# Fourteen pairs instead of thirteen in the down projection of a hybrid decoder layer

## The chip, the cores and the metric

The kernel runs on one core of one Trainium2 chip. The core has five engines with a queue of instructions each: TensorE (PE, matrix products; PEld is its loading of the stationary operand), VectorE (DVE), ScalarE (ACT), GpSimd (POOL) and SyncE (SP), which here issues nearly all DMA transfers. The metric is the device time of one execution in microseconds (us), and the median over several executions is what counts. Matrix products are summed in eight PSUM banks; everything else lies in SBUF, 128 partitions wide.

## The reference

One decoder layer in fp32 over 256 positions of width 2048:

```python
h    = rmsnorm(x, pre_mix_gain)
proj = h @ w_in                                   # 2048 x 6144
o_sb = head_rmsnorm(stick_breaking_attention(q_sb, k_sb, v_sb))        # 8 heads
o_dl = head_rmsnorm(dilated_attention(rope(q_dl), rope(k_dl), v_dl))   # 8 heads
x    = x + rmsnorm(concat(o_sb, o_dl) @ w_out, post_mix_gain)
h    = rmsnorm(x, pre_ffn_gain)
u    = causal_conv3(h @ w_up) + conv_b            # 2048 x 11008
y    = gelu(u[:, :5504]) * u[:, 5504:]
x    = x + rmsnorm(y @ w_down, post_ffn_gain)     # 5504 x 2048
```

What concerns the change is the last product, `y @ w_down`: 43 blocks of 128 along the 5504 rows, each against 2048 columns, for two blocks of 128 positions.

## The kernel before, in words

**Products in parts.** A weight arrives in fp32 (`raw`, a ring of five buffers of 128 × 1024), ACT rounds it to its high part `wh` (L88), and DVE subtracts that to get the low part `wl` (L93); both have rings of four. The activations are split in the same way. Each product is then three matmuls into one bank: high by high, low by high, high by low (in down L621, L622, L623).

**Stages.** v and qk with the attention of the heads between them, out, up, down, in this order on PE. In each of the first 55 steps behind the seventh, `presum` is called once (L895).

**Down.** The output has two column halves (`cp` 0 and 1) of 1024 columns. A half takes the 43 blocks of rows in two ways. A *single* (`ONE`) is one block: four products, 12 matmuls, one raw tile of 1024 columns. A *pair* (`PAIR`) is two blocks by a scheme of the Strassen kind: seven products instead of eight, 21 matmuls. It has four units: Rb (two products), Ra (one, 512 wide), T13 and T24 (two each). T13 is a sum of weights that `presum` has formed during attention: it loads two pieces of `w_dn` (b12 and t13), adds them on DVE (L575) and writes the result to DRAM (`t13_kept`), from where down reads it as any weight. T24 is formed in down by two additions of 512 columns on DVE (L604, L606). The activations of a pair (`yp`, seven matrices) are formed in up, those of a single (`yt`) as well. `prepare` runs three units ahead of `multiply`.

The order comes from `_down_plan`: with 13 pairs there are 17 singles. Half 0 opens with two singles, then pairs with singles spread between them (rounded down), and both halves end with four singles (`HELD`). In half 0 pairs 0 and 1, and 6 and 7, stand side by side; in half 1 a single follows each pair. Where the order isn't written out, the framework places each instruction on its engine; `pin` and `keep_in_program_order` fix it.

**Between and behind the halves.** `combine` (L630 to L634) adds the pairs' products of banks 1, 5, 6 and 7; `close` (L641) adds a bank of singles to that, ACT squares the sum for the last norm (L436), and the result is scaled by the gain `gbc` (L643). In half 1 the four held singles run bank by bank (2, 3, 4, and 8 in two pieces), so that each bank is closed while PE works on the next; L680 (`put`) applies the norm and adds x1, and SP writes the output. `x1p` is a piece of x1 that ACT copies to PSUM (L693) for it.

**Small things.** `along_rows` (L311) turns a column of factors into rows by a product with a matrix of ones; it is used in the first norm and, behind the first pieces of up, in the second (`r2ps`). Up's `convolved` computes a gate and a value in the tiles `cv0` and `cv1`; a pair's sums lie in the tile `pair`.

Of the kernel before, what the change touches and what calls it, by code (L numbers as in the profile page):

```python
# [16 lines left out]
P = 128  # L17
D = 2048
S = 256
# [14 lines left out]
NPAIR = 13  # L34
# [17 lines left out]
def layer_kernel(ctx: ExitStack, tc: tile.TileContext, a, out: bass.AP):  # L52
# [12 lines left out]
    def pin(ins):  # L65

        if pinned[0]:
            tc.keep_in_program_order(ins)
        return ins
# [81 lines left out]
    def rstd_of(v, n):  # L151

        l = small.tile([P, n], F32, tag=f"rl{n}", name="rl")
        A.activation(l, v, AF.Ln)
        r0 = small.tile([P, n], F32, tag=f"r0{n}", name="r0")
        A.activation(r0, l, AF.Exp, scale=-0.5)
        q = small.tile([P, n], F32, tag=f"rq{n}", name="rq")
# [3 lines left out]
        r = small.tile([P, n], F32, tag=f"rr{n}", name="rr")  # L161
        V.tensor_tensor(r, r0, q, op=ALU.mult)
        return r
# [131 lines left out]
    ones = cpool.tile([P, P], F32, name="ones")  # L295
    G.memset(ones, 1.0)
# [8 lines left out]
    def along_rows(r, name):  # L305

        ps = ps_at.tile([P, S], F32, tag="at", name=name)
        for t in range(2):
            dg = small.tile([P, P], F32, tag="diag", name="diag", bufs=1)
            V.tensor_scalar(dg, ident, r[t], None, op0=ALU.mult)  # L310
            T.matmul(ps[:, t * P:(t + 1) * P], ones, dg, start=True, stop=True)  # L311
        return ps

    def first_norm():

        V.tensor_copy(tri, cst[:, C_TRI:C_TRI + P])
        G.tensor_copy(idb, ident)
        G.tensor_copy(mskb, cst[:, C_MSK:C_MSK + P])
        ss = small.tile([P, 2], F32, tag="ssx", name="ssx", bufs=1)
        for t in range(2):  # L320
            A.activation(gbc, x1[:, t, :], AF.Square, accum_out=ss[:, t:t + 1])
        v0 = small.tile([P, 2], F32, tag="vx", name="vx", bufs=1)
        V.tensor_scalar(v0, ss, 1.0 / D, EPS, op0=ALU.mult, op1=ALU.add)
        V.tensor_copy(rstd1, rstd_of(v0, 2))
        rps = along_rows((rstd1[:, 0:1], rstd1[:, 1:2]), "rps")
# [9 lines left out]
    def finish_head(h, at, den):  # L335
# [7 lines left out]
        hs = small.tile([P, 2], F32, tag="hs", name="hs")  # L343
# [3 lines left out]
        v = small.tile([P, 2], F32, tag="hv", name="hv")  # L347
        if den is None:
            V.tensor_scalar(v, hs, 1.0 / P, EPS, op0=ALU.mult, op1=ALU.add)
        else:  # L350

            e2 = small.tile([P, 2], F32, tag="e2", name="e2")
# [42 lines left out]
    def dilated_head(h, qk):  # L395
# [12 lines left out]
        m = small.tile([P, 2], F32, tag="m", name="m")  # L408
        den = small.tile([P, 2], F32, tag="den", name="den")
# [77 lines left out]
    def convolved(ps, p, s):  # L487
# [5 lines left out]
        cv = phB.tile([P, S], F32, tag=f"cv{s}", name="cv", bufs=1)  # L493
# [6 lines left out]
        else:  # L500
            m, odd = p // (FT // NPAIR), p % (FT // NPAIR)
            if p in SINGLES:
                n = SINGLES.index(p)
                V.tensor_tensor(cv, gate[0], cv, op=ALU.mult)
# [3 lines left out]
            if odd == 0:  # L508
                pair[0] = phB.tile([P, 7, P], F32, tag="pair", name="pair", bufs=1)
            y = pair[0]  # L510
            V.tensor_tensor(y[:, 2 * odd:2 * odd + 2, :], gate[0], cv, op=ALU.mult)
# [9 lines left out]
    class Down:  # L521
# [42 lines left out]
        def presum(self, tick):  # L564


            pair, odd = divmod(tick, 2)
            if not odd and 0 <= pair - 2 < len(self.presums):
                t13, _, kept = self.summed[pair - 2]
                tc.keep_in_program_order(nc.sync.dma_start(kept, t13))  # L570
            if odd and 0 <= pair - 1 < len(self.presums):
                t13, one, _ = self.summed[pair - 1]
# [3 lines left out]
            if not odd and pair < len(self.presums):  # L576
# [68 lines left out]
        def run(self):  # L645
# [254 lines left out]
    V.tensor_scalar(gbc, gbc, -0.5, None, op0=ALU.mult)  # L900
# [75 lines left out]
```

## Time and profile before

| | |
|---|---|
| median of three runs | 1117.7 us (1117.26 to 1117.78) |
| profiled execution: its own time | 1117.35 us |
| its span | 1115.6 us |
| granted clock | 0.998 |
| PE busy | 1103.6 us, 5855 matmuls |
| DVE, ACT busy | 880.6 us, 659.1 us |

By the trace, attention runs to about 312 us, the output projection to 397, up from 414 to 887.9, half 0 of down to 997.35, half 1 to the last matmul at 1106.8, and the last output leaves by 1115.6.

The rows in the prediction are of these kinds. A timeline row has the start, the duration, engine, line, operation, output <- inputs, shapes and how many equal ones it stands for; brackets name the idle time ahead of it and what ended it. A group row has a shape, its count, busy time and mean nanoseconds of one, then the engine's idle time ahead of such instructions and its releasers. A row of waits has the total, the number and the longest. A row of windows has, behind the stretch and its length, each engine's busy time with its instructions, then PE's clock, the share of DMA and GB/s.

### The profile page before, as it was taken

The numbers are of one execution on the slowest core, as the hardware profiler recorded it, in microseconds if no ns is written. First come the engines' busy times: TensorE is split into PE (matmuls) and PEld (weight loads), VectorE is DVE, ScalarE is ACT, GpSimd is POOL, SyncE is SP. The second block draws the span as 40 slices with busy tenths as digits, with TensorE's granted clock in tenths as the row PEclk, the third lists the DMA queues.
The fourth block names the chain that finished last, engine by engine and source line by source line (L and its number), as shares of the span: only waits on it lengthen the run. The fifth ranks groups of instructions, "written<-read, shape, count | busy, mean of one in ns | idle before, by whom it ended". The sixth has DMA issues, their size and how long they took to land.

```text
span 1115.6 us, 16305 instructions
## 1 busy us (share of the span) xinstructions
PE 1103.6 (99%) x5855; PEld 941.3 (84%) x5855; DVE 880.6 (79%) x1373; ACT 659.1 (59%) x1041; POOL 3.3 (0%) x10
## 2 busy tenths in 40 slices
PE   9999999999999999999999999999999999999996
PEld 6888888888888888888888888888888888888885
DVE  6577776777776589878888878888878898889887
ACT  6656665655654376655555555555555566666664
POOL 0000000000000000000000000000000000000000
PEclk9999999999999999999999999999999999999999
DMA  9977778878879756555555555555555577777775
GB/s 319 369 254 272 256 250 269 300 251 277 274 259 320 274 199 211 189 189 189 189 189 185 188 184 187 185 188 187 188 189 189 173 252 244 249 223 246 245 238 206
DMA packets 75393, 257.79 MB, mean 231 GB/s; under 512 B 8496, under 2 KB 9648, under 8 KB 74544
## 3 DMA queue, kind: packets, MB, share of 16 engines
q1 hardware_dynamic: 75168, 256.74, 68.9%
q8 instruction: 46, 0.75, 0.3%
q14 instruction: 35, 0.29, 0.1%
q10 hardware_dynamic: 144, 0.01, 0.0%
HBM read 238.89 MB, written 17.83 MB: 230 GB/s over the span
## 4 chain that ended last, share of the span: by engine, by line
PE 98%; DVE 0%; DMA 0%; ACT 0%; issue 0%; DVEq 0%; SPq 0%; ACTq 0%
PE mmu L101 28%; PE mmu L104 14%; PE mmqk L101 11%; PE p L622 7%; PE p L621 7%; PE p L623 6%; PE mmqk L104 5%; PE mmv L144 3%; PE mmv L147 3%; PE mmo L143 3%; PE mmv L143 3%; PE mmo L144 3%; PE mmo L147 3%; PE mmu L110 1%; DMA raw<-in_w_v 0%; PE po L341 0%
## 5 line engine op out<-in xcount | busy, mean ns | idle before, releaser
L88 ACT CAST wh<-raw 128x1024 fp32r<-128x1024 f32 (+1 forms) x408 | 415.1, 1024 | 356.4 <-PE mmu L101 190.1
L93 DVE TENSOR_TENSOR wl<-raw,wh 128x1024 fp32r<-128x1024 f32 (+1 forms) x408 | 482.5, 1189 | 165.2 <-ACT wh L88 160.6
L101 PE MATMUL mmu<-hT,wh 128*128 128x512 f32 x1344 | 340.9, 396 | 0.0
L101 PEld LDWEIGHTS mmu<-hT,wh 128*128 128x128 f32 x1344 | 240.2, 188 | 45.6
L104 PEld LDWEIGHTS mmu<-hT,wl 128*128 128x128 f32 x1344 | 182.8, 189 | 15.2
L104 PE MATMUL mmu<-hT,wl 128*128 128x256 f32 x1344 | 186.4, 281 | 0.0
L101 PE MATMUL mmqk<-hT,wh 128*128 128x512 f32 x512 | 133.0, 401 | 0.0
L101 PEld LDWEIGHTS mmqk<-hT,wh 128*128 128x128 f32 x512 | 92.0, 188 | 17.2
L104 PEld LDWEIGHTS mmqk<-hT,wl 128*128 128x128 f32 x512 | 69.9, 188 | 5.8
L622 PE MATMUL p<-wh,yp 128*128 128x512 f32 x182 | 71.7, 394 | 0.0
L621 PE MATMUL p<-wh,yp 128*128 128x512 f32 x182 | 71.3, 392 | 0.0
L104 PE MATMUL mmqk<-hT,wl 128*128 128x256 f32 x512 | 71.1, 281 | 0.0
L623 PE MATMUL p<-wl,yp 128*128 128x512 f32 x182 | 70.8, 389 | 0.0
L622 PE MATMUL p<-wh,yt 128*128 128x512 f32 (+1 forms) x140 | 54.2, 387 | 0.0
L621 PE MATMUL p<-wh,yt 128*128 128x512 f32 (+1 forms) x140 | 54.0, 385 | 0.0
L623 PE MATMUL p<-wl,yt 128*128 128x512 f32 (+1 forms) x140 | 53.3, 382 | 0.0
L494 ACT ACTIVATE cv<-u,par 128x256 f32<-128x256 f32 x86 | 51.5, 598 | 2.4 <-DVE u L492 2.3
L143 PE MATMUL mmv<-wh,hT 128*128 128x512 f32 x128 | 51.6, 405 | 0.4 <-ACT hT L225 0.4
L144 PE MATMUL mmv<-wh,hT 128*128 128x512 f32 x128 | 50.8, 397 | 0.2 <-DVE hT L226 0.2
L143 PE MATMUL mmo<-wh,mix 128*128 128x512 f32 x128 | 50.4, 394 | 0.0
L88 ACT CAST wh<-room 128x1024 fp32r<-128x1024 f32 x26 | 27.3, 1050 | 38.6 <-PE p L622 36.4
L144 PE MATMUL mmo<-wh,mix 128*128 128x512 f32 x128 | 49.9, 390 | 0.0
(175 smaller groups left out, 1218.6 us busy)
## 6 DMA issues: line engine op xcount, KB each, us to landing
raw<-in_w_up SPq DMA_DIRECT2D x172, 512.0 KB, 4.4
raw<-in_w_qk SPq DMA_DIRECT2D x64, 512.0 KB, 4.9
raw<-in_w_dn SPq DMA_DIRECT2D x60, 512.0 KB, 4.6
raw<-in_w_o SPq DMA_DIRECT2D x32, 512.0 KB, 5.0
raw<-in_w_v SPq DMA_DIRECT2D x28, 512.0 KB, 5.6
t<-in_w_dn SPq DMA_DIRECT2D x26, 512.0 KB, 5.7
t_kept<-t SPq DMA_DIRECT2D x26, 512.0 KB, 3.9
raw<-t_kept SPq DMA_DIRECT2D x26, 512.0 KB, 4.4
```

Of the source, the lines that this page charges most:

```text
L88: pin(A.copy(wh, raw))
L93: pin(V.tensor_tensor(wl, raw, wh.bitcast(F32), op=ALU.subtract))
L101: T.matmul(ps, wh[:, j * P:(j + 1) * P], h[:, k, :, :], start=(k == 0), stop=False, skip_group_check=True)
L104: T.matmul(ps[:, 0, :], wl[:, j * P:(j + 1) * P], h[:, k, 0, :], start=False, stop=(k == KT - 1), skip_group_check=True)
L110: T.matmul(ps[:, part, :], parts[k // 8][low][:, k % 8 * P:(k % 8 + 1) * P], h[:, k, part, :], skip_group_check=True, **kw)
L143: T.matmul(ps[t], hi[:, k, tc_], ws, start=(first and i == 0 and j == 0), stop=False)
L144: T.matmul(ps[t], lo[:, k, tc_], ws, start=False, stop=False)
L147: T.matmul(ps[t], hi[:, k, tc_], wl[:, j * 512:(j + 1) * 512], start=False, stop=(last and i == len(parts) - 1 and j == n - 1))
L494: A.activation(cv, u, AF.Identity, scale=cw(2), bias=par[:, P_CB + f:P_CB + f + 1])
L621: T.matmul(ps, yh, wh[:, cs], start=key not in self.begun, stop=False)
L622: T.matmul(ps, yl, wh[:, cs], start=False, stop=False)
L623: T.matmul(ps, yh, wl[:, cs], start=False, stop=self.left[key] == 0)
```

## The change

- NPAIR goes from 13 to 14, so 15 singles are left in each half. Half 0 opens with three singles, and the others are spread by rounding up: side by side stand now pairs 2 and 3, 4 and 5, 6 and 7, 9 and 10, 11 and 12 in half 0, 4 and 5 and 9 and 10 in half 1, and in both halves the last pair stands directly ahead of the four held singles.
- `presum` spreads 28 sums over 52 steps with its own lags, instead of one per two steps.
- The attention's small tiles (`rl`, `r0`, `rq`, `rr`, `hs`, `hv`, `e2`, `m`, `den`) move from the pool `small`, which lives to the end, to `apool`, which ends ahead of up. Both have four buffers for them.
- `ones` and the diagonal share one tile of the early pool, and for the second norm a new tile is taken in the buffer `pair`, and POOL fills it again.
- Up's value half lies inside the tile `pair`, and its gate in a tile of its own.
- The gain's scaling by −0.5 moves from ahead of down to the middle of half 0.
- The copies `x1p` move ahead of the products of bank 3.

```diff
-NPAIR = 13
+NPAIR = 14
+SUM_STEPS = 52
...
-    plan = [("one", left.pop(0)) for _ in range(0 if cp else 2)]
+    plan = [("one", left.pop(0)) for _ in range(0 if cp else 3)]
     spread = len(left) - HELD
     for m in range(NPAIR):
         plan.append(("pair", m))
-        plan += [("one", left.pop(0)) for _ in range((m + 1) * spread // NPAIR - m * spread // NPAIR)]
+        plan += [("one", left.pop(0)) for _ in range(-(-(m + 1) * spread // NPAIR) + (-m * spread // NPAIR))]
...
-        l = small.tile([P, n], F32, tag=f"rl{n}", name="rl")
+        l = apool.tile([P, n], F32, tag=f"rl{n}", name="rl", bufs=4)
...
-    ones = cpool.tile([P, P], F32, name="ones")
-    G.memset(ones, 1.0)
+    ones = apool.tile([P, 2 * P], F32, name="ones", bufs=1)
+    G.memset(ones[:, 0:P], 1.0)
...
-            dg = small.tile([P, P], F32, tag="diag", name="diag", bufs=1)
+            dg = ones[:, P:2 * P]
             V.tensor_scalar(dg, ident, r[t], None, op0=ALU.mult)
-            T.matmul(ps[:, t * P:(t + 1) * P], ones, dg, start=True, stop=True)
+            T.matmul(ps[:, t * P:(t + 1) * P], ones[:, 0:P], dg, start=True, stop=True)
...
         rs = [sq.newton(*sq.mean(t)) for t in range(2)]
+        ones = phB.tile([P, 2 * P], F32, tag="pair", name="ones", bufs=1, padded_shape=[P, 7 * P])
+        G.memset(ones[:, 0:P], 1.0)
         r2B = cpool.tile([P, S], F32, name="r2B")
-        V.tensor_scalar(r2B, along_rows(rs, "r2ps"), -0.5, None, op0=ALU.mult)
+        V.tensor_scalar(r2B, along_rows(rs, "r2ps", ones), -0.5, None, op0=ALU.mult)
...
-        cv = phB.tile([P, S], F32, tag=f"cv{s}", name="cv", bufs=1)
+        m, odd = p // (FT // NPAIR), p % (FT // NPAIR)
+        if s == 0:
+            cv = phB.tile([P, S], F32, tag="gate", name="gate", bufs=1)
+        else:
+            if p in SINGLES or odd == 0:
+                pair[0] = phB.tile([P, 7, P], F32, tag="pair", name="pair", bufs=1)
+            at = 0 if p in SINGLES else 2 * odd
+            cv = pair[0][:, at:at + 2, :].rearrange("p a b -> p (a b)")
...
-            pair, odd = divmod(tick, 2)
-            if not odd and 0 <= pair - 2 < len(self.presums):
-                t13, _, kept = self.summed[pair - 2]
+            def due(lag):
+                n, k = len(self.presums), tick - lag
+                return next((p for p in range(n) if SUM_STEPS * p // n == k), None)
+
+            pair = due(3)
+            if pair is not None:
+                t13, _, kept = self.summed[pair]
                 tc.keep_in_program_order(nc.sync.dma_start(kept, t13))
...
                     self.prepare(u + 1 + self.AHEAD)
+                    if cp == 0 and u == n // 2:
+                        tc.keep_in_program_order(V.tensor_scalar(gbc, gbc, -0.5, None, op0=ALU.mult))
                     self.multiply(u)
...
             take2(V)
+            pinned[0] = True
+            for i in range(2):
+                pin(A.copy(x1p[i], x1s[1][:, i * 512:(i + 1) * 512]))
             products(3)
             take3 = self.close(1, 3)
-            for i in range(2):
-                A.copy(x1p[i], x1s[1][:, i * 512:(i + 1) * 512])
-            pinned[0] = True
...
-    V.tensor_scalar(gbc, gbc, -0.5, None, op0=ALU.mult)
```

In the changed kernel the lines of down stand further on: L94 is the subtraction L93 of before, L616 and L618 are L604 and L606, L633 to L635 are the matmuls L621 to L623, L643 to L646 the combining additions, L653 `close`, L655 the scaling by the gain, L667 the scaling of `gbc`, L680 the subtraction of bank 8, L694 `put`.

The first place is DVE in the middle of half 0, where pairs 6 and 7 stand side by side in both kernels. Before (`wl<-room` is the low part of T24, `wl<-raw` of 512 columns that of Ra):

```order
L93 TENSOR_TENSOR wl<-raw,wh 128x1024
L93 TENSOR_TENSOR wl<-room,wh 128x1024
L604 TENSOR_TENSOR room<-raw 128x512
L93 TENSOR_TENSOR wl<-raw,wh 128x1024
L93 TENSOR_TENSOR wl<-raw,wh 128x512
L606 TENSOR_TENSOR room<-room,raw 128x512
L93 TENSOR_TENSOR wl<-raw,wh 128x1024
L93 TENSOR_TENSOR wl<-room,wh 128x1024
L93 TENSOR_TENSOR wl<-raw,wh 128x1024 x2
L604 TENSOR_TENSOR room<-raw 128x512
```

and in the changed kernel, from the last unit of pair 7 on:

```order
L94 TENSOR_TENSOR wl<-raw,wh 128x1024
L94 TENSOR_TENSOR wl<-room,wh 128x1024
L667 TENSOR_SCALAR room<-room 128x2048
L94 TENSOR_TENSOR wl<-raw,wh 128x1024 x2
L616 TENSOR_TENSOR room<-raw 128x512
L94 TENSOR_TENSOR wl<-raw,wh 128x512
```

Between T24 of pair 7 and the single behind it the scaling of the gain now stands.

The second place is DVE at the end of half 1, from the first low part behind T24 of the last pair (`room` is the result, `p6`, `p5`, `p7`, `p2`, `p8`, `p3` are banks). Before:

```order
L93 TENSOR_TENSOR wl_10716<-raw_10649,wh_10714 128x1024
L93 TENSOR_TENSOR wl_10723<-raw_10658,wh_10721 128x1024
L93 TENSOR_TENSOR wl_10733<-raw_10708,wh_10731 128x1024
L631 TENSOR_TENSOR room_9005<-p6_9932,room_9005 128x512
L93 TENSOR_TENSOR wl_10748<-raw_10710,wh_10746 128x1024
L632 TENSOR_TENSOR room_9005<-p5_9930,room_9005 128x512
L633 TENSOR_TENSOR room_9005<-p7_9931,room_9005 128x512
L93 TENSOR_TENSOR wl_10764<-raw_10712,wh_10762 128x1024
L634 TENSOR_TENSOR room_9005<-p5_9930,room_9005 128x512
L641 TENSOR_TENSOR room_9005<-p2_9936,room_9005 128x512
L666 TENSOR_TENSOR room_9005<-room_9005,p8_9937 128x512
L643 TENSOR_TENSOR room_9005<-room_9005 128x512
```

and now:

```order
L94 TENSOR_TENSOR wl_10735<-raw_10670,wh_10733 128x1024
L94 TENSOR_TENSOR wl_10742<-raw_10679,wh_10740 128x1024
L94 TENSOR_TENSOR wl_10752<-raw_10729,wh_10750 128x1024
L643 TENSOR_TENSOR room_8990<-p6_9926,room_8990 128x512
L94 TENSOR_TENSOR wl_10767<-raw_10731,wh_10765 128x1024
L644 TENSOR_TENSOR room_8990<-p5_9924,room_8990 128x512
L653 TENSOR_TENSOR room_8990<-p2_9930,room_8990 128x512
L645 TENSOR_TENSOR room_8990<-p7_9925,room_8990 128x512
L646 TENSOR_TENSOR room_8990<-p5_9924,room_8990 128x512
L655 TENSOR_TENSOR room_8990<-room_8990 128x512
L680 TENSOR_TENSOR room_8990<-room_8990,p8_9931 128x512
L653 TENSOR_TENSOR room_8990<-p3_9929,room_8990 128x512
```

Five low parts stood here, the first that of a single; now there are the four of the held units. Two of the combining additions stand behind the closing of bank 2, and the scaling ahead of the subtraction of bank 8.

More of the change, by code (lines that the diff above doesn't have):

```diff
@@ L160, in rstd_of @@
         V.tensor_scalar(q, q, -0.5, 1.5, op0=ALU.mult, op1=ALU.add)
-        r = small.tile([P, n], F32, tag=f"rr{n}", name="rr")
+        r = apool.tile([P, n], F32, tag=f"rr{n}", name="rr", bufs=4)
         V.tensor_tensor(r, r0, q, op=ALU.mult)
@@ L324, in first_norm @@
         V.tensor_copy(rstd1, rstd_of(v0, 2))
[L325 removed]
+        rps = along_rows((rstd1[:, 0:1], rstd1[:, 1:2]), "rps", ones)
         V.tensor_scalar(rB[:, 0, :], rps, SCALE, None, op0=ALU.mult)
@@ L342, in finish_head @@
         T.matmul(po[:, 1, :], at[:, 2 * P:3 * P], vt[:, 1, hc], start=False, stop=True)
-        hs = small.tile([P, 2], F32, tag="hs", name="hs")
+        hs = apool.tile([P, 2], F32, tag="hs", name="hs", bufs=4)
         for t in range(2):
@@ L346, in finish_head @@
             A.activation(jk, po[:, t, :], AF.Square, accum_out=hs[:, t:t + 1])
-        v = small.tile([P, 2], F32, tag="hv", name="hv")
+        v = apool.tile([P, 2], F32, tag="hv", name="hv", bufs=4)
         if den is None:
@@ L350, in finish_head @@
         else:
-            e2 = small.tile([P, 2], F32, tag="e2", name="e2")
+            e2 = apool.tile([P, 2], F32, tag="e2", name="e2", bufs=4)
             V.scalar_tensor_tensor(e2, den, EPS, den, op0=ALU.mult, op1=ALU.mult)
@@ L564, in presum @@
         def presum(self, tick):
-            pair, odd = divmod(tick, 2)
-            if not odd and 0 <= pair - 2 < len(self.presums):
-                t13, _, kept = self.summed[pair - 2]
+            def due(lag):
[4 more added lines that the diff above has]
+                t13, _, kept = self.summed[pair]
                 tc.keep_in_program_order(nc.sync.dma_start(kept, t13))
-            if odd and 0 <= pair - 1 < len(self.presums):
-                t13, one, _ = self.summed[pair - 1]
+            pair = due(2)
+            if pair is not None:
+                t13, one, _ = self.summed[pair]
                 b12 = one.rearrange("p (o c) -> p o c", o=1).broadcast_to([P, 2, 512])
@@ L575, in presum @@
                 tc.keep_in_program_order(V.tensor_tensor(two, b12, two, op=ALU.add))
-            if not odd and pair < len(self.presums):
+            pair = due(0)
+            if pair is not None:
                 one, two, kept = self.presums[pair]
```

16 lines of the change are left out of this document (6 added, 10 removed).

## The prediction

> **What bounds the kernel now.** First the page: busy time, granted clock by slice, and the chain that ended last.
>
> ```profile
> span 1115.6 us, 16305 instructions
> PE 1103.6 (99%) x5855; PEld 941.3 (84%) x5855; DVE 880.6 (79%) x1373; ACT 659.1 (59%) x1041; POOL 3.3 (0%) x10
> ...
> PEclk9999999999999999999999999999999999999999
> ...
> PE 98%; DVE 0%; DMA 0%; ACT 0%; issue 0%; DVEq 0%; SPq 0%; ACTq 0%
> ```
>
> TensorE is busy or being fed nearly all the time, its clock is full, and the chain is PE for 98%. A busy share of 99% can hide short stalls, so I read next what PE waited for:
>
> ```profile
> PE idle L234 <- DVE warm L231: 1.2, 1, 1.2
> PE pth L803 <- DVE x L795: 1.2, 1, 1.2
> ```
>
> The one wait above 1 us behind the start is at the step from the output projection to up. In down there is none of that size. So the time is the number of matmuls times their pitch, plus what DVE does alone at the end. The pitch is not the mean duration. In the PE timeline a single (12 matmuls) and a pair (21) lie between these starts:
>
> ```profile
> 918.38 0.39 PE L621 MATMUL p<-wh,yt 128*128 128x512 f32 x1
> ...
> 921.13 0.39 PE L621 MATMUL p<-wh,yp 128*128 128x512 f32 x1
> ...
> 925.94 0.39 PE L621 MATMUL p<-wh,yt 128*128 128x512 f32 x1
> ```
>
> A single takes 2.75 us and a pair 4.81 us: 0.229 us a matmul, though each row says 0.39, because neighbours overlap.
>
> **Matmuls removed: −1.37 us.** The groups by line and shape:
>
> ```profile
> L621 PE MATMUL p<-wh,yp 128*128 128x512 f32 x182 | 71.3, 392 | 0.0
> ...
> L621 PE MATMUL p<-wh,yt 128*128 128x512 f32 x132 | 51.7, 392 | 0.0
> ```
>
> One pair more in each column half makes the pair products 196 (28 × 7); two singles fewer in each make the single ones 132 − 16 = 116. Per line that is 2 fewer, on three lines 6, and 6 × 0.229 = 1.37 us. With 0.39 one would write 2.3 us, which the pitch forbids.
>
> **The opening of down: −0.24 us.** DVE (L900, L93), ACT (table load) and PE there:
>
> ```profile
> 887.93 0.40 PE L621 MATMUL p<-wh,yt 128*128 128x512 f32 x1
> ...
> 897.10 0.40 PE L622 MATMUL p<-wh,yp 128*128 128x512 f32 x1
> 897.42 0.51 PE L623 MATMUL p<-wl,yp 128*128 128x512 f32 x1
> 897.77 0.40 PE L621 MATMUL p<-wh,yp 128*128 128x512 f32 x1
> ...
> 898.47 0.39 PE L621 MATMUL p<-wh,yp 128*128 128x512 f32 x1
> ```
> ```profile
> 893.23 1.22 DVE L900 TENSOR_SCALAR room<-room 128x2048 f32<-128x2048 f32 x1
> ...
> 896.15 1.23 DVE L93 TENSOR_TENSOR wl<-room,wh 128x1024 fp32r<-128x1024 f32 x1
> ```
> ```profile
> 893.77 1.28 ACT L902 ACT_TABLE_LOAD   x1
> ```
>
> From 887.93 to 898.47 lie two singles and a pair: 45 × 0.229 = 10.30 us, but it takes 10.54. The lost 0.24 is the low part of pair 0's last unit, ready at 896.15 + 1.23 = 897.38, just as PE asks for it. A third single puts 2.75 us of PE work ahead of that unit against 1.14 us of DVE work (cadence below), and the 1.22 us gain scaling L900 is gone from there. I take the whole 0.24; bounds 0 and 0.24.
>
> **The new memset and the diagonal: +0.15 us.** POOL now fills `ones` again in the second norm.
>
> ```profile
> 420.93 0.42 PE L311 MATMUL r2ps<-diag,ones 128*128 128x128 f32 x2
> ```
> ```profile
> 416.38 0.19 ACT L436 ACTIVATION_READ_ACCUMULATOR jks<-x 128x1 f32 x1
> ```
> ```profile
> L296 POOL MEMSET ones<- x1: 206/206/206, 0.9 to 0.9; 128x128 f32 x1
> ```
>
> The tile takes the buffer of the squares' scratch, so the memset waits for the last square, 416.57, and takes 0.2 us as at the start. PE reads it at 420.93: 4.2 us of cover, and POOL has nothing else queued there. If the cover were gone, PE would stand for the lateness. But the matmul now waits on more semaphores, the last being the diagonal's own, and the PE queue behind it is the up stage. No row prices that; bounds 0 and 0.3, I take the middle.
>
> **Attention and up: 0.** Two more presums are two more of these additions, and 2.6 MB more traffic (768 KB in and 512 KB out, twice):
>
> ```profile
> L575 DVE TENSOR_TENSOR t<-b,t 128x1024 f32<-128x1024 f32 x26 | 31.7, 1220 | 0.0
> ```
> ```profile
> 0.00:312.00 312.00, 310.24 (x1683) 263.75 (x1684) 219.03 (x390) 187.57 (x356) 1.14 (x8) 1.00 0.81 282
> 414.00:887.90 473.90, 473.90 (x2699) 412.70 (x2698) 392.73 (x644) 279.65 (x422) 0.00 (x0) 1.00 0.58 189
> ```
>
> In the attention stage DVE is busy 219 of 312 us and DMA 81%, so 2.4 us and 1% more bytes find room; DVE is the cover, and without it PE would lose the 2.4 us. The small tiles keep four buffers. In up, DVE's 393 of 474 us covers the extra pair's sums, and the half and the sum now live in the buffer that the sum alone had, behind readers that have long ended.
>
> **Down's steady state: +0.05 us.** The place with two pairs side by side and no single between them exists once in the middle of before:
>
> ```profile
> 937.34 1.23 DVE L93 TENSOR_TENSOR wl<-room,wh 128x1024 fp32r<-128x1024 f32 x1 [0.87 <-ACT wh L88]
> ...
> 942.70 1.23 DVE L93 TENSOR_TENSOR wl<-room,wh 128x1024 fp32r<-128x1024 f32 x1
> ...
> 997.23 1.88 DVE L641 TENSOR_TENSOR room<-p,room 128x512 f32<-128x512 f32 x3
> ...
> 1090.53 3.50 DVE L93 TENSOR_TENSOR wl<-raw,wh 128x1024 fp32r<-128x1024 f32 x3 [0.22 <-ACT wh L88]
> ```
> ```profile
> 940.13 0.39 PE L623 MATMUL p<-wl,yp 128*128 128x512 f32 x1
> ...
> 944.94 0.39 PE L623 MATMUL p<-wl,yp 128*128 128x512 f32 x1
> ...
> 946.31 0.39 PE L623 MATMUL p<-wl,yt 128*128 128x512 f32 x1
> ```
>
> Behind a single, the last low part of a pair ends at 938.57, 1.56 us ahead of the matmul that reads it (940.13); behind a pair at 943.93, 1.01 us ahead (944.94). PE doesn't wait. DVE starts a 1024-wide subtraction every (3.50 − 1.22) / 2 = 1.14 us and a 512-wide operation every (1.88 − 0.68) / 2 = 0.60, so two pairs and a single cost it 2 × (3 × 1.14 + 3 × 0.60) + 1.14 = 11.6 us against PE's 2 × 4.81 + 2.75 = 12.37. The change has five such places in the first half and two in the second, each followed by time to recover. The gain scaling (1.22 us long, about 1.14 as a step) now stands behind the third of them. The single's low part there ends at 945.06 or so (one step behind 943.93), 1.25 us ahead of 946.31: 1.14 of that is used up. I put 0.05; bounds 0 and 0.6 (if the third place starts with 0.5 less).
>
> **Between the halves: +0.15 us.** Four singles, not five, separate the last pair from the next half:
>
> ```profile
> 998.04 0.39 PE L621 MATMUL p<-wh,yp 128*128 128x512 f32 x1
> ```
>
> PE may start a bank of the next half only when its sum has been taken. The three closings at 997.23 are banks 3, 2 and 8: the first ends at 997.23 + 0.68 = 997.91, and PE starts bank 3 again at 998.04, with 0.1 us to spare. One single less moves loads and subtractions ahead of it up to 0.35 us later. Bounds 0 and 0.35; middle.
>
> **The end: +0.6 us.** Before, a single stands between the last pair and the four held units, and DVE combines the pair products behind it. PE starts the pair's last unit at 1091.42:
>
> ```profile
> 1091.42 0.39 PE L621 MATMUL p<-wh,yp 128*128 128x512 f32 x1
> ...
> 1100.81 0.39 PE L623 MATMUL p<-wl,yt 128*128 128x512 f32 x1
> ```
> ```profile
> 1101.35 0.68 DVE L641 TENSOR_TENSOR room<-p,room 128x512 f32<-128x512 f32 x1
> ...
> 1106.81 0.42 DVE L641 TENSOR_TENSOR room<-p,room 128x256 f32<-128x256 f32 x1 [0.21 <-PE p L623]
> ```
>
> Counted from that unit, after has four low parts (start −0.89, as 1090.53 is now; 4 × 1.14), four combining additions, the first closing, a scaling and the subtraction of bank 8, about 0.60 to 0.68 each: 7 steps, 4.4 us. DVE is then free at −0.89 + 4.56 + 4.4 = 8.0. PE has bank 3 ready, one single (2.75) earlier than before, at 1100.81 + 0.39 − 1091.42 − 2.75 = 7.0. From this closing to the last one the chain ran 5.46 us, 0.21 of it waiting for PE, so the last closing comes at 8.0 + 5.25 = 13.25; before, less the single, at 1106.81 − 1091.42 − 2.75 = 12.64. That is +0.6. The serial work behind it is unchanged. Bounds 0 (if the additions find gaps) and 1.0 (the whole lateness 8.0 − 7.0). Moving the copies x1p earlier only uses ACT's idle time.
>
> **Sum.** −1.37 − 0.24 + 0.15 + 0.05 + 0.15 + 0.6 = −0.66 us. The profiled execution took 1117.35 us (1115.6 span, 1.75 around it), so 1116.7; the median of the runs is 0.35 above it, hence 1117.7 − 0.66 = 1117.0.
>
> **Rivals.**
>
> *All covers hold.* The end and the boundary lose nothing: −1.61, 1116.1. For it: DVE idles 0.87 us per pair. Against: at the end DVE runs without a gap. Chance 0.15.
>
> *DVE sets the pace* (the slower side). If a next operation started only when the one before had ended, a pair would cost 3 × 1.22 + 3 × 0.68 = 5.7 us of DVE, 0.9 more than PE's 4.81, and a single would give back 2.75 − 1.22 = 1.53. The cover of 1.56 at pair 2 would be 0.65, 0.4 and 0.1 behind the three double places, and the gain scaling would then stop PE for about 1.1 us; the end grows by 0.5 at the longer steps. −0.66 + 1.1 + 0.5 = +0.9, 1118.6. It decides from the place where cover falls under the scaling's 1.14. For it: 1.56 falls to 1.01 at the place that exists. Against: starts are 1.14 apart, not 1.22. Chance 0.13. The Trainium skill, "VectorE: DVE Perf Modes", section "The DRAIN you can't avoid", says that the next op does not start until the pipe is empty, which would be this rival; it adds that an op that isn't held starts earlier, and the 1.14 us in this trace agrees with that clause.
>
> *The kept sums land late.* Two pairs in a row take 2.6 MB in 9.6 us.
>
> ```profile
> L604 DVE TENSOR_TENSOR room<-raw 128x512 f32<-128x512 f32 x26 | 17.8, 685 | 1.2 <-DMA raw<-t_kept 0.7 <-PE mmu L104 0.5
> ```
>
> L604 has already waited 0.7 us for these loads. At 0.5 us in each of the five new double places it is +2.5, 1119.5 with the rest. Against: in the double place of before, 937 to 946 us, PE never waited. Chance 0.06.
>
> *Something in attention moves.* Other lags of the presums reorder SP's queue there; one stall like L803's 1.2 us, twice, gives 1119.4. Chance 0.04; and 0.02 for a hidden gain that I don't see.
>
> **How the numbers follow.** Forecast 0.6, its own range 1116.3 to 1117.9. For 8 in 10: low 1115.8 (all covers hold, 1116.1, less 0.3 for the spread of the medians), high 1118.6 (every term at its upper end, −1.37 + 0 + 0.3 + 0.6 + 0.35 + 1.0 = +0.9, and the second rival). A measurement of this kernel tells about 0.2%, 2.2 us, from no change: 1115.5 to 1119.9. Only the hidden gain with part of the first rival lies below, 0.05; the kept sums and attention at their worst above, 0.06; the same 0.89.
>
> **What would show it.** Six fewer matmuls, at 0.229; the low part of pair 0's last unit over 1 us early; no gap ahead of r2ps; the gain scaling with PE going on behind it; in the end DVE without idle time up to the closing of bank 3 and no wait ahead of the last closing. It is wrong if PE shows gaps in the double places, if L616 waits for DMA, or if attention and up don't end at the same time as before.

## The result, and the profile after

The changed kernel takes 1123.29 us (median of five runs, 1122.85 to 1124.62) against 1117.7: a ratio of 1.0053 with a 95% interval of 1.0042 to 1.0064. It is 5.6 us slower; forecast was 0.7 us faster. The page of the changed kernel, span, busy time, clock and chain:

```profile
span 1121.5 us, 16346 instructions
PE 1108.6 (99%) x5849; PEld 939.9 (84%) x5849; DVE 888.8 (79%) x1386; ACT 661.9 (59%) x1044; POOL 3.5 (0%) x11
...
PEclk9999999999999999999999999999999999999998
...
PE 95%; DVE 2%; DMA 2%; ACT 1%; issue 0%; DVEq 0%; SPq 0%; ACTq 0%
```

Six matmuls fewer, as forecast, and yet TensorE is busy 5.0 us longer, at a granted clock of 0.997 (0.998 before). The span is 5.9 us longer. Where it went is read from the starts of stages in the two traces. First the output projection: two starts in each trace, with 240 matmuls between them; before, then after.

```profile
342.09 0.39 PE L143 MATMUL mmo<-wh,mix 128*128 128x512 f32 x1
...
396.49 0.39 PE L143 MATMUL mmo<-wh,mix 128*128 128x512 f32 x1
```
```profile
342.45 0.39 PE L144 MATMUL mmo<-wh,mix 128*128 128x512 f32 x1
...
398.22 0.39 PE L144 MATMUL mmo<-wh,mix 128*128 128x512 f32 x1
```

54.40 us became 55.77: 0.227 us a matmul became 0.232. Nothing of the projection's code was changed. In down one single (12 matmuls) of the changed kernel:

```profile
892.48 0.39 PE L634 MATMUL p<-wh,yt 128*128 128x512 f32 x1
...
895.28 0.40 PE L633 MATMUL p<-wh,yt 128*128 128x512 f32 x1
```

It takes 2.80 us where it took 2.75: 0.233 a matmul instead of 0.229. The time until the output projection is over (the start of the matmul behind it) is 1.75 us longer (397.40 to 399.15), from there to down it is equal (490.53 in both), down from its first to its last matmul is 3.63 us longer (218.56 to 222.19), and what follows the last matmul 0.60 longer (9.07 to 9.67). Together 5.98, which is the difference of the spans.

In down there are waits as well. PE's and DVE's waits in the changed kernel (total, times, longest):

```profile
PE p L635 <- DVE wl L94: 0.4, 1, 0.4
```
```profile
DVE room L616 <- DMA raw<-t_kept: 6.2, 4, 1.7
```

And the place where DVE waits, as the timelines of DVE and PE show it:

```profile
899.40 0.69 DVE L616 TENSOR_TENSOR room<-raw 128x512 f32<-128x512 f32 x1 [1.50 <-DMA raw<-t_kept]
900.12 0.69 DVE L618 TENSOR_TENSOR room<-room,raw 128x512 f32<-128x512 f32 x1
900.73 1.22 DVE L94 TENSOR_TENSOR wl<-room,wh 128x1024 fp32r<-128x1024 f32 x1
...
909.65 0.69 DVE L616 TENSOR_TENSOR room<-raw 128x512 f32<-128x512 f32 x1 [1.53 <-DMA raw<-t_kept]
910.26 2.95 DVE L94 TENSOR_TENSOR wl<-raw,wh 128x1024 fp32r<-128x1024 f32 x3
...
916.64 0.69 DVE L616 TENSOR_TENSOR room<-raw 128x512 f32<-128x512 f32 x1 [1.69 <-DMA raw<-t_kept]
917.25 1.22 DVE L94 TENSOR_TENSOR wl<-room,wh 128x1024 fp32r<-128x1024 f32 x1
```
```profile
902.04 0.47 PE L635 MATMUL p<-wl,yp 128*128 128x512 f32 x1
...
910.99 0.40 PE L634 MATMUL p<-wh,yt 128*128 128x512 f32 x1
911.53 0.50 PE L635 MATMUL p<-wl,yt 128*128 128x512 f32 x1
...
917.70 0.40 PE L634 MATMUL p<-wh,yp 128*128 128x512 f32 x1
918.53 0.50 PE L635 MATMUL p<-wl,yp 128*128 128x512 f32 x1 [0.43 <-DVE wl L94]
```

L616 adds the kept sum of a pair, and stands in DVE's queue ahead of low parts that PE needs first. It waits for the load, they wait behind it, and PE starts L635 0.31 us late at 911.53 and 0.59 late at 918.53. The first of these is the single behind pair 1, the second the last unit of pair 2, which pair 3 follows directly. With 0.1 behind each it is 1.1 us.

### The profile page after: what moved, and what is told of

It reads as the page before. It is cut to its first block, busy times and chain, and to the rows that moved or that the text cites. A ratio compares the mean times of both kernels' runs of the same rounds, so it can differ in the third digit from the quotient of the medians.

```text
span 1121.5 us, 16346 instructions
## 1 busy us (share of the span) xinstructions
PE 1108.6 (99%) x5849; PEld 939.9 (84%) x5849; DVE 888.8 (79%) x1386; ACT 661.9 (59%) x1044; POOL 3.5 (0%) x11
## 4 chain that ended last, share of the span: by engine, by line
PE 95%; DVE 2%; DMA 2%; ACT 1%; issue 0%; DVEq 0%; SPq 0%; ACTq 0%
PE mmu L102 28%; PE mmu L105 14%; PE mmqk L102 11%; PE p L635 6%; PE p L633 6%; PE p L634 6%; PE mmqk L105 5%; PE mmo L144 3%; PE mmo L148 3%; PE mmo L145 3%; PE mmv L145 3%; PE mmv L148 3%; PE mmv L144 3%; DMA raw<-t_kept 1%; PE mmu L111 1%; DVE wl L94 1%
## 5 line engine op out<-in xcount | busy, mean ns | idle before, releaser
L94 DVE TENSOR_TENSOR wl<-raw,wh 128x1024 fp32r<-128x1024 f32 (+1 forms) x410 | 483.3, 1186 | 162.2 <-ACT wh L89 160.5
L635 PE MATMUL p<-wl,yp 128*128 128x512 f32 x196 | 77.7, 396 | 0.4 <-DVE wl L94 0.4
L634 PE MATMUL p<-wh,yp 128*128 128x512 f32 x196 | 77.5, 395 | 0.0
L633 PE MATMUL p<-wh,yp 128*128 128x512 f32 x196 | 77.5, 395 | 0.0
L633 PE MATMUL p<-wh,yt 128*128 128x512 f32 (+1 forms) x124 | 48.1, 388 | 0.0
L634 PE MATMUL p<-wh,yt 128*128 128x512 f32 (+1 forms) x124 | 48.1, 388 | 0.0
L635 PE MATMUL p<-wl,yt 128*128 128x512 f32 (+1 forms) x124 | 47.8, 388 | 0.1
L635 PEld LDWEIGHTS p<-wl,yp 128*128 128x128 f32 x196 | 36.8, 188 | 10.0 <-DVE wl L94 1.1
```

Source lines behind the costliest of these rows:

```text
L94: pin(V.tensor_tensor(wl, raw, wh.bitcast(F32), op=ALU.subtract))
L633: T.matmul(ps, yh, wh[:, cs], start=key not in self.begun, stop=False)
L634: T.matmul(ps, yl, wh[:, cs], start=False, stop=False)
L635: T.matmul(ps, yh, wl[:, cs], start=False, stop=self.left[key] == 0)
```

## The experiments

The pitch changed in two stages whose code is the same, so I looked at what the change moves there without touching it: the place of the tiles in SBUF, as the allocator gives them. Offsets are counted from here on within lines of 512 bytes of a partition (the address modulo 512). `small` became 1664 bytes per partition smaller and 512 bytes of `ones` left the pool ahead of the rings. `wh` and `wl` moved by 512 bytes and start at byte 448 of a line in both kernels. `mix` moved from 448 to 320, `yt` and `yp` from 384 to 256. `hT` stays at 416. Theory A: the pitch depends on these offsets. Theory B: it depends on the load beside PE.

### Moving yt and yp alone

Unused space ahead of `yt`, 128 bytes in the changed kernel (as shown), 384 and 64 in the one before:

```diff
+                phB.tile([P, 32], F32, name="pad", bufs=1)
                 yt = [phB.tile([P, len(SINGLES), S], F32R, name=f"yt{i}", bufs=1) for i in range(2)]
```

after_yt_back:

> The changed kernel with 128 bytes per partition of unused space ahead of yt and yp, so that down's activations start at byte 384 of a 512-byte line again, as in before (256 in the changed kernel); instructions and order stay. Theory A, the pitch of the matmuls depends on the offset of the operand that PE reads: down's pitch goes from 0.233 to 0.229 us, 960 x 0.004 = 3.8 us less, 1119.5; the output projection keeps its 0.232 (mix isn't moved). Theory B, the pitch grew because of what runs beside (more double pairs, DVE and DMA load): no change, 1123.3.

before_yt_moved:

> The kernel before with 384 bytes of unused space at the same place, so that yt and yp start at byte 256 as in the changed kernel; nothing else. Theory A: down's pitch goes from 0.229 to 0.233, 966 x 0.004 = +3.9 us, 1121.6, with thirteen pairs and no other part of the change. Theory B: 1117.7.

before_yt_same:

> The kernel before with 64 bytes of unused space, so that yt and yp start at byte 448, where wh and wl also start; in the output projection, where mix and wh both start at 448, the pitch was 0.227. Theory A in the form 'equal offsets are fastest': down's pitch 0.227, 966 x 0.002 = 1.9 us less, 1115.8. If only the offset of yt itself counts and 384 is best: 1117.7 or slower. Theory B: 1117.7.

| run | yt, yp at byte | pitch in down, ns | median, us | ratio to before (95%) |
|---|---|---|---|---|
| before | 384 | 229 | 1117.37 | |
| changed kernel | 256 | 233 | 1123.29 | 1.0053 (1.0042 to 1.0064) |
| after_yt_back | 384 | 229 | 1120.56 | 1.0028 (1.0018 to 1.0038) |
| before_yt_moved | 256 | 233 | 1121.49 | 1.0038 (1.0023 to 1.0053) |
| before_yt_same | 448 | 227 | 1115.45 | 0.9983 (0.9973 to 0.9992) |

The pitch is the median distance of starts of 512-wide matmuls. The changed kernel's ratio is to its own comparison, 1117.7; beside each later group of runs the kernel before had a median of 1117.3 to 1117.6. The kernel before with nothing but its activations moved loses 4.1 us; moved the other way it gains 1.9. A single of before_yt_moved, and one of before_yt_same:

```profile
918.74 0.40 PE L621 MATMUL p<-wh,yt 128*128 128x512 f32 x1
...
921.54 0.40 PE L621 MATMUL p<-wh,yp 128*128 128x512 f32 x1
```
```profile
918.24 0.39 PE L621 MATMUL p<-wh,yt 128*128 128x512 f32 x1
...
920.96 0.39 PE L621 MATMUL p<-wh,yp 128*128 128x512 f32 x1
```

2.80 and 2.72 us, with the same instructions in the same order. That decides for theory A, and theory B falls: thirteen pairs with the old singles have the slow pitch too. In after_yt_back down takes 218.20 us instead of 222.19, so the pitch cost 3.99 us there, more than the 3.63 that down lost in all; without it down is 0.36 shorter than before. before_yt_moved confirms the size: its down takes 222.57 us against 218.56. The medians of the changed kernel and of after_yt_back differ by only 2.7 us (1123.29, 1120.56): the profiled execution of after_yt_back was the fastest of eight (1119.07; the slowest took 1121.39). What made the others longer is not shown.

### Which offset: the distance between the two operands

before_yt_zero, before_yt_416 and before_yt_64 are the same edit with 128, 32 and 192 bytes. before_wh_moved moves the rings `raw`, `wh` and `wl` by 64 bytes to byte 0, and `yt` to byte 0 with 128 bytes:

```diff
-    rstd1 = cpool.tile([P, 2], F32, name="rstd1")
+    r2B_ = cpool.tile([P, S], F32, name="r2B")
+    rstd1 = r2B_[:, 0:2]
+    cpool.tile([P, 24], F32, name="pad0")
...
-        ss = small.tile([P, 2], F32, tag="ssx", name="ssx", bufs=1)
+        ss = r2B_[:, 2:4]
...
-        v0 = small.tile([P, 2], F32, tag="vx", name="vx", bufs=1)
+        v0 = r2B_[:, 4:6]
```

> The kernel before with 128 bytes of unused space, so that yt and yp start at byte 0 of a 512-byte line, while wh and wl stay at 448. If equality with wh decides: a pitch in down above 0.227, like the 0.229 at a distance of 64 bytes. If the start at a whole line decides: 0.227 or less. Time by the one 1117.4, by the other 1115.4 or less.

> The kernel before with 32 bytes of unused space: yt and yp at byte 416, 32 below wh, which is the distance of hT and wh in v and qk (0.234). By the distance: 0.233 to 0.234 in down, 1121.7 to 1122.5. By the nearness to 448 alone, between 384 (0.229) and 448 (0.227): 0.228, 1116.5.

> The kernel before with 192 bytes of unused space: yt and yp at byte 64, 128 above wh. mix in the changed kernel stood 128 below wh (0.232); 64 above gave 0.233. By the distance without its sign: 0.232, 1120.6; if only the side counts (above is slow): 0.233, 1121.7.

> The kernel before with raw, wh and wl 64 bytes further on, at byte 0 of a 512-byte line, and yt and yp at byte 0 too; mix (448) and hT (416) stay. If the distance between the operands decides: down 0.227 (equal, though yt at 0 alone gave 0.233), out 0.229 (mix 64 bytes below wh, as yt was in before). If the place of the stationary operand alone decides: down 0.233, out 0.227. If a whole-line start helps: down below 0.227.

The pitch of 512-wide matmuls with `wh` or `wl` as the moving operand (the 512-wide one; the stationary one is 128 wide), against the distance of the stationary operand's start from the moving one's in a 512-byte line:

| distance, bytes | stationary and moving at | pitch, ns | where |
|---|---|---|---|
| 0 | 448, 448 | 227 | out of before; down of before_yt_same |
| 0 | 0, 0 | 227 | down of before_wh_moved |
| −64 | 384, 448 | 229 | down of before |
| −64 | 448, 0 | 229 | out of before_wh_moved |
| −32 | 416, 448 | 234 | v of before; down of before_yt_416 |
| −96 | 416, 0 | 231 | v of before_wh_moved |
| −128 | 320, 448 | 232 | out of the changed kernel |
| −192 | 256, 448 | 233 | down of the changed kernel and of before_yt_moved |
| +64 | 0, 448 | 233 | down of before_yt_zero |
| +128 | 64, 448 | 232 | down of before_yt_64 |

One execution of each of the four gave 1121.73, 1121.43, 1120.47 and 1114.87 us in the order of the texts above. Byte 0 is slow for `yt` when `wh` is at 448, and as fast as 448 when `wh` is at 0 too; and `mix`, which before_wh_moved left alone, became slower when `wh` moved away from it. So the distance decides, not the place of one operand, and a whole line is nothing special. Its sign counts too: 64 bytes below is 229, 64 above 233. A single of before_wh_moved takes 2.72 us:

```profile
917.63 0.39 PE L623 MATMUL p<-wh,yt 128*128 128x512 f32 x1
...
920.35 0.39 PE L623 MATMUL p<-wh,yp 128*128 128x512 f32 x1
```

Why the distance counts, no run shows; the steps between −32, −64 and −96 follow no simple line. Nor do the runs tell that 512 bytes is the period: −192 and +64 lie 256 apart and both give 233, −128 and +128 both 232, so a period of 256 would fit as well.

### hT at the same offset

```diff
+    rstd1 = cpool.tile([P, 2], F32, name="rstd1")
     hT2 = cpool.tile([P, KT, 2, S], F32R, tag="hT", name="hT")
...
-    rstd1 = cpool.tile([P, 2], F32, name="rstd1")
```

> The kernel before with the small tile rstd1 placed ahead of hT, so that hT starts at byte 448 of a 512-byte line, as wh and wl do, and not at 416; nothing else moves. Theory A in the form 'equal offsets are fastest': the 512-wide matmuls of v, qk and up go from 0.232 to 0.234 down to 0.227: up 1334 x 0.006 = 8.0, qk 512 x 0.005 = 2.6, v 384 x 0.007 = 2.7, together 13 us less, 1104.4. In the form 'multiples of 64 are fast': some gain of the same sign, less than 13. Theory B: 1117.7.

1111.47 us, 0.9947 (0.993 to 0.9963): 5.9 us less, by 32 bytes. In v the pitch went from 234 to 227. In up, where `hT` moves and `wh` is stationary, eight 512-wide and eight 256-wide matmuls of the kernel before, and of this one:

```profile
600.97 2.03 PE L101 MATMUL mmu<-hT,wh 128*128 128x512 f32 x8
602.84 1.11 PE L104 MATMUL mmu<-hT,wl 128*128 128x256 f32 x8
603.78 2.03 PE L101 MATMUL mmu<-hT,wh 128*128 128x512 f32 x8
```
```profile
600.00 2.00 PE L101 MATMUL mmu<-hT,wh 128*128 128x512 f32 x8
601.85 1.11 PE L104 MATMUL mmu<-hT,wl 128*128 128x256 f32 x8
602.80 2.00 PE L101 MATMUL mmu<-hT,wh 128*128 128x512 f32 x8
```

A round of 2.81 us became 2.80 here, and this adds up: over the whole stage the 1344 512-wide matmuls take 4.3 us less (233.4 to 230.2 ns on the mean) and the 256-wide ones 1.0 more (118.4 to 119.1), and up is 3.3 us shorter from its first matmul to down. I had counted on 0.227 there and 13 us: the rule that v and down follow holds in up only in part, and for 256 columns not at all.

### Fourteen against thirteen pairs at an equal pitch

after_same puts `mix`, `yt`, `yp` and `hT` of the changed kernel at byte 448; before_same does it in the kernel before.

```diff
-            e2 = apool.tile([P, 2], F32, tag="e2", name="e2", bufs=4)
+            e2 = small.tile([P, 2], F32, tag="e2", name="e2")
...
+                phB.tile([P, 16], F32, name="pad", bufs=1)
...
+    rstd1 = cpool.tile([P, 2], F32, name="rstd1")
     hT2 = cpool.tile([P, KT, 2, S], F32R, tag="hT", name="hT")
```

> The changed kernel with yt and yp, mix and hT all at byte 448 of a 512-byte line, where wh and wl start (64 bytes ahead of yt, the tiles e2 back in the pool small, rstd1 ahead of hT). Theory A, equal offsets are fastest: out 0.232 to 0.227 (-1.8), down 0.233 to 0.227 (960 x 0.006 = -5.8), and what hT brought in before_hT_same (-5.9): 1123.3 - 13.5 = 1109.8, with the stalls of the opening left. If the effects share a cause and don't add: 1112 to 1118.

> The kernel before with yt, yp and hT at byte 448 together. If the two gains measured one by one add: 1117.4 - 1.9 - 5.9 = 1109.6. Against after_same this is thirteen against fourteen pairs with the pitch made equal: by the matmuls alone fourteen would be 1.4 us faster; with what the traces show of the opening (+1.1) and the end (+0.56) the two are equal within 0.5 us.

before_same: 1109.2 us, 0.9927 (0.9911 to 0.9944); the two gains add. after_same: 1112.06 us (1110.32 to 1113.18), 0.9951 (0.9936 to 0.9965), where I had expected 1109.8. The output projection has the pitch of before again, 227, with the changed order of the presums, so its 1.75 us were the place of `mix`. With the pitch out of the way the change still costs about 2.9 us in the medians: in the traces down is 217.99 us long against 216.63, although six matmuls fewer should have made it 215.27, and the end is 0.59 longer. The rest is in attention (0.5) and in the spread of the executions. The late starts in down cost 2.7 us here and 1.1 in the changed kernel. That a faster PE reaches the same low parts earlier fits this; no run tests it alone. PE's waits in after_same:

```profile
PE p L635 <- DVE wl L94: 0.7, 1, 0.7
PE p L633 <- DVE room L653: 0.3, 1, 0.3
```

The first is the opening again (0.90 late at 910 us, 0.28 at 903), the second the start of half 1, where PE waits for the closing of a bank (0.43 late).

### Where the stalls of the opening come from

after_gbc_late keeps the changed kernel with `yt` at 384 and issues the gain's 1 MB load later:

```diff
-    nc.sync.dma_start(gbc, a["gpost"][1:2, :].partition_broadcast(P))
...
+                    if cp == 0 and u == 16:
+                        tc.keep_in_program_order(nc.sync.dma_start(gbc, a["gpost"][1:2, :].partition_broadcast(P)))
```

> The changed kernel with yt back at byte 384 (as in after_yt_back, 1120.56) and the 1 MB load of the last gain issued at unit 16 of down's first half instead of ahead of its first loads. Theory C, the stalls behind down's opening come from the kept sums of pairs 1 to 3, which share the DMA engines with that load: L616 no longer waits 1.5 us for them there, PE's stall of 0.6 us near 917 goes, 1119.9. Theory D, the loads are late because the ring of five raw buffers is freed late by the order with three singles: the stall stays, 1120.6.

1120.82 us, 1.0031 (1.0019 to 1.0042), no better than after_yt_back; PE's late starts only moved (0.39 at 918, 0.52 at 931, 0.52 at 935). By itself this run doesn't rule the load out: it now went out at 914.57 and took 8.0 us, beside the first of these late starts. The trace of the changed kernel says more. SyncE issues there:

```profile
889.87 0.33 SPq L913 DMA_DIRECT2D room<-in_gpost  x1
...
894.28 0.33 SPq L600 DMA_DIRECT2D raw<-t_kept  x1
...
904.85 0.33 SPq L600 DMA_DIRECT2D raw<-t_kept  x1
...
912.64 0.33 SPq L600 DMA_DIRECT2D raw<-t_kept  x1
```

The gain's load took 7.5 us there and had landed at 897.4, before the two kept sums were asked for (904.85 and 912.64) whose waits made PE late at 911.53 and 918.53. So theory C falls for these two; only the load of 894.28, for the low part that came just in time, ran beside it.

after_pin and the four runs behind it start from after_same. after_pin holds DVE's order in down as the program writes it:

```diff
+            pinned[0] = True
             later = []
...
-                    V.tensor_tensor(t24[:, 0:512], t13[:, 0:512], rb[:, 512:], op=ALU.add)
+                    pin(V.tensor_tensor(t24[:, 0:512], t13[:, 0:512], rb[:, 512:], op=ALU.add))
```

> after_same (1112.06) with down's low parts and the two additions for T24 held in the order of the program on DVE, so that the first addition (L616), which needs the kept sum of its pair, stands behind the low part of its own pair's first unit and no longer ahead of the last low part of the pair before and of singles. Theory E, the stalls of the opening come from that place in DVE's queue: the waits of PE for low parts at 903 and 910 us (0.28 and 0.90, with the 0.1 behind each 1.4 together) go, 1110.7. Theory D, the kept sums simply land too late for their own use, as the ring of raw buffers is full: the waits stay under other names, 1112.

1111.09 us, 0.9945 (0.9929 to 0.9962). The waits of DVE for kept sums and of PE now:

```profile
DVE room L616 <- DMA raw<-t_kept: 0.7, 2, 0.4
```
```profile
PE p L633 <- ACT wh L89: 1.5, 2, 0.8
```

In after_same DVE waited 7.2 us for kept sums, now 0.7, and PE's waits for low parts at 903 and 910 us are gone: the place of L616 in DVE's queue made them, and theory D, that the sums land too late whatever the order, doesn't fit the 0.7. But the same pins hold ACT's casts in order, and PE waits twice for those instead (1.0 us late at 888, 0.8 at 995). So 1.0 us is gained where 1.4 was expected, and this run mends one thing by breaking another.

The next two change the places of the singles only. after_old_plan takes both rules of before, after_floor only the second, the rounding:

```diff
-    plan = [("one", left.pop(0)) for _ in range(0 if cp else 3)]
+    plan = [("one", left.pop(0)) for _ in range(0 if cp else 2)]
...
-        plan += [("one", left.pop(0)) for _ in range(-(-(m + 1) * spread // NPAIR) + (-m * spread // NPAIR))]
+        plan += [("one", left.pop(0)) for _ in range((m + 1) * spread // NPAIR - m * spread // NPAIR)]
```

> after_same with the rules of before for the singles: two open the first half, and the rest are spread rounded down, so that one single stands between the last pair and the held units. Fourteen pairs stay. By the reading of the end, the time from the last matmul to the end goes from 9.66 back to 9.07 us (-0.6), and the wait of PE at the start of half 1 (0.43) goes. By the reading of the opening, the stalls there change: if three singles cause them, -1.4 and 1109.6; if the double places cause them (pairs 0 and 1 now stand side by side), they stay or grow, 1111 or more.

> after_same (1112.06) with three opening singles kept and the other singles spread rounded down, without any pinning. after_old_plan (two singles, rounded down) took 1108.45. If the third single in the opening causes the stalls there, they stay: 1111; if the places of the others cause them, the time is that of after_old_plan within 0.5 us.

after_old_plan 1108.45 us, 0.9922 (0.9908 to 0.9937); after_floor 1108.67 us, 0.9921 (0.9905 to 0.9938). Down takes 215.61 and 215.43 us, the end 8.87 in both. Of after_floor's waits of PE none lies in down; behind the start of the program these two are the longest:

```profile
PE pth L817 <- DVE x L809: 1.2, 1, 1.2
PE mmv L144 <- ACT hT L227: 0.4, 1, 0.4
```

So three opening singles are harmless, and the rounding decides. Rounded up, a single stands behind pair 0 and behind pair 1, and the framework puts L616 of the next pair early in DVE's queue: in after_same that of pair 2 stands ahead of the single's low part and waits 1.33 us (901.45), that of pair 3 ahead of the last low part of pair 2 and waits 1.85 (908.60). Rounded down, pairs 0 and 1 stand side by side, and both stand behind these low parts and wait for nothing (899.72 and 904.74). DVE still waits 2.3 us for kept sums, 2.0 of it at 987.82, at the change of the halves, but not ahead of anything that PE needs at once. One single again separates the last pair from the held units. The double places, which I had taken for the risk, cost nothing in this order, six of them in the first half.

after_pin_floor and after_pin_old put the pins and these places together:

> after_pin with three opening singles and the others spread rounded down: one single between the last pair and the held units again. Against after_pin only the places of singles differ: -0.6 at the end and -0.4 at the start of half 1, against the cost of pairs 0 and 1 side by side. With theory E 1109.7.

> after_pin with the rules of before for the singles (two open, rounded down). With no stall left in down fourteen pairs would beat before_same (1109.2) by 6 x 0.227 = 1.4, 1107.8. If DVE cannot keep up with the faster pitch in the double places, 1109 to 1111.

1112.59 us (0.9958, 0.9943 to 0.9973) and 1112.91 us (0.9963, 0.9948 to 0.9978): slower than without pins, with PE waiting for ACT's casts 2.2 and 3.5 us in all. The forecasts of 1109.7 and 1107.8 were wrong, because the pins cost more than the order was worth.

The best versions, after_floor and after_old_plan, beat the kernel before by 0.8%. Of that, 0.7% is the offsets alone (before_same). Against before_same fourteen pairs with the old rounding are 0.5 to 0.8 us faster in the medians; the intervals of the ratios overlap, but in the traces down is 1.0 to 1.2 us shorter and the end 0.2.

## Why the prediction was wrong

**Attention and up: 0.** This is the step that failed, together with the pitch that the next step took over. I asked of the moved small tiles only whether they keep their four buffers, and of the memory only who waits for whom. The moves shifted `mix` by 128 bytes and `yt` and `yp` by 128 within a line of 512. The output projection lost 1.75 us, which I had in no term, and down about 4.0.

**Matmuls removed: −1.37 us.** The count was right, 196 and 116, but the step took the pitch of before as fixed:

```profile
L633 PE MATMUL p<-wh,yp 128*128 128x512 f32 x196 | 77.5, 395 | 0.0
...
L633 PE MATMUL p<-wh,yt 128*128 128x512 f32 x116 | 45.9, 395 | 0.0
```

The mean duration went from 392 to 395 ns, which looks like nothing; the pitch went from 229 to 233, and down's 960 matmuls lost about 4.0 us by it (3.99 in after_yt_back, 4.01 in before_yt_moved). The stages of before have different pitches with the same shapes, 227, 229 and 234, and the prediction doesn't ask why. The Trainium skill, "TensorE: Matmul & The Clock Gate", section "Back-to-back issue gap", gives N / 2.4 + 2.5 ns at full clock for the gap of isolated matmuls, which for 512 columns is 216 ns, and about 131 ns a matmul for a sustained stream of 512-column matmuls with their weight loads. No run here came under 227, and neither figure has a term for what moved.

**The opening of down: −0.24 us.** Wrong in sign. I took it that the third single puts PE's work ahead of pair 0's last low part. It does, but DVE does that part behind L616 and L618 of the next pair, which waited 1.50 us for a load (899.40): the part ends at 901.95, and PE reads it at 902.04, again just in time, not over 1 us early. The same happens twice more and costs 1.1 us. DVE's order in the changed kernel, shown ahead of the prediction at two places, is not shown there for the opening.

**The kept sums land late** was a rival with 0.06 and 2.5 us. Its mechanism is real, L616 waiting for t_kept, but it strikes near the opening only: at the single behind pair 1 (0.31 late) and in a new double place, pairs 2 and 3 (0.59). It costs 1.1 us in the changed kernel, not 2.5. With that, three of the prediction's own signs of being wrong showed: a gap of PE in a double place, L616 waiting for DMA, and an output projection that ended later.

**Down's steady state: +0.05 us.** Right: no wait of PE in the later double places nor at the gain's scaling. DVE starts a 1024-wide subtraction every 1.14 us there too (the three at 1098.48, below), so the rival in which DVE sets the pace fell. The Trainium skill's rule that the next op waits for an empty pipe ("VectorE: DVE Perf Modes", section "The DRAIN you can't avoid") holds here only with its own exception for ops that aren't held.

**Between the halves: +0.15 us.** The changed kernel has no such wait; at the faster pitch of after_same it has, 0.43 us late, for the reason given. It was a matter of who is faster.

**The new memset: +0.15 us.** Nothing: from up's first matmul (401.04 before, 402.80 now) to r2ps both traces take 19.88 us, and from r2ps to the start of down 467.00.

**The end: +0.6 us.** Right in sum, 0.60 by the traces, and in part by luck. DVE and PE in the changed kernel there:

```profile
1098.48 3.50 DVE L94 TENSOR_TENSOR wl<-raw,wh 128x1024 fp32r<-128x1024 f32 x3 [0.21 <-ACT wh L89]
...
1107.44 0.68 DVE L653 TENSOR_TENSOR room<-p,room 128x512 f32<-128x512 f32 x1
...
1112.51 0.42 DVE L653 TENSOR_TENSOR room<-p,room 128x256 f32<-128x256 f32 x1
```
```profile
1099.45 0.39 PE L633 MATMUL p<-wh,yp 128*128 128x512 f32 x1
```

The closing of bank 3 starts 7.99 us behind the start of the pair's last unit (forecast 8.0), and the last closing at 13.06 (forecast 13.25) has no wait ahead of it. So DVE's chain was read rightly, but the last closing is 0.42 later than before (13.06 against 12.64), not 0.61. From it to the end it takes 9.04 us against 8.75, where I had the serial work unchanged; where these 0.29 us arise is open.

With the measured terms the sum is: pitch +1.75 and +4.0, matmuls −1.37, stalls of the opening +1.1, the end +0.6, which is +6.1 against 5.9 in the span. Without the pitch it would have been +0.3, about 1.0 above the forecast of −0.66, and mostly by the opening. That is for these two profiled executions at the pitch of before; at the faster pitch of after_same the stalls are longer, and the change costs 2.9.

## What to carry to other kernels

When a change moves tiles, compare the addresses that the allocator gives, not only the instructions: a stage whose code is untouched can change its pitch. Where the same shape of matmul has different pitches in different stages, ask why before taking one of them as fixed; here starting both operands of a matmul at the same byte of a 512-byte line was worth 0.7%, several times the six matmuls that the fourteenth pair saves (1.4 us). And an instruction that waits for a load costs what is queued behind it, so a queue that the framework orders has to be read at every place where loads run short.

## What the runs showed of the hardware

The pitch of 512-wide fp32r matmuls, with the clock full and no wait, lay between 227 and 234 ns by the distance of the two operands' starts, counted within 512 bytes of SBUF (a period of 256 would fit as well): 227 at distance 0 (at bytes 448 and 0 alike), 229 at −64, 231 to 234 at the other six distances measured. With `hT` moving and the weights stationary, distance 0 gave 230 instead of 233 in up on the mean, while the 256-wide matmuls there went from 117 to 120 ns in the median. What in the chip makes it so is open.
